# A two-layer hybrid trunk on one core: the first modulation group k tile by k tile, and the next layer's preparation behind the last residual sums

## The chip, the core and the metric

The kernel runs on one core of a Trainium2 chip. The metric is device time in microseconds of one execution; the profile's span, from the first to the last instruction, is a little shorter. The engines are TensorE (PE; its weight loads are listed as PEld), VectorE (DVE), ScalarE (ACT), GpSimd (POOL) and SyncE (SP), which issues nearly all DMAs. Each engine works through its own queue in order; the queues wait for each other by semaphores. VectorE, ScalarE and TensorE work on SBUF and PSUM, GpSimd on SBUF.

## The reference: what is computed

x is 256 tokens by 2048 float32; there are two layers. The core of a layer is:

```python
shift, scale, gate = split(silu(c) @ w_ada[l] + b_ada[l], 3)        # 2048 -> 3 x 2048, for one row c
h = rms_norm(x, norm_w[l]) * (1 + scale) + shift
(gq, gk, gv, glr, gz, dq, dk, dv, da, db, dz, aq, ak, av, az) = split(h @ w_in[l])   # 2048 -> 7704
o_gla  = gated linear attention(gq, gk, gv, glr), normed, times silu(gz)      # 512 wide
o_gdn  = gated delta rule(dq, dk, dv, da, db), normed, times silu(dz)         # 512 wide
o_diff = differential softmax attention(aq, ak, av), normed, times silu(az)   # 1024 wide
x = x + gate * (concat(o_gla, o_gdn, o_diff) @ w_out[l])                      # 2048 -> 2048
```

## The kernel before, in words

x lies transposed: 128 features on the partitions, 16 k tiles of 128 features, 256 tokens along the row. All large weights come from memory once, as tiles of 128x1024 float32 (512 KB), through one pool of six buffers (`wraw`, tag `raw`) that projection weights (`raw`), output weights (`raw`) and modulation weights (`rawa`) share in program order.

Products keep float32 accuracy by splitting both factors: `weights` (L292 to L303) issues the DMA on SP, ScalarE rounds to the fast format (`wh`, L300) and VectorE takes the rest (`wl`, L301), into three buffers each. Each product is then three matmuls: high by high, high by low, low by high. The modulated input is split in the same way into `hh` (ScalarE, L389) and `hl` (VectorE, L390).

The modulation vectors come from `ada_group`: a group is eight VectorE products of a 128x1024 tile with the broadcast `c_row`, each with a running sum (L325), and four small ScalarE finishes (L337). Groups 0 to 7 of a layer give scale and shift of two k tiles each, groups 8 to 11 the gate. Layer 0's first group uses two separate buffers `fr`, the others `raw` buffers. `ada_to(n)` emits products up to mark n (eight per group, 96 per layer); `ADA_BY` and `PACE` say how far the products have to be at the end of each projection step and how they are spread over the 48 columns of the output projection. In a product's place in the program order the scheduler may still move it: `high_priority(offset=AHEAD)` lets it go before other work.

A layer begins with `rstd_rows` (ones-matmuls over the squares, mean, power, two diagonal matrices on ScalarE, a matmul that spreads the row factors over the partitions, a copy to `rb`), then `modulate` for pairs of k tiles (hn, hh, hl: L388 to L390), then `project` for each entry of `STEPS`, a range of output blocks and of k tiles. Layer 0's first step is blocks 18 to 27 (ten of 512 columns) over k tiles 0 and 1: its first chunk of weights holds two blocks for k tile 0, the second the same blocks for k tile 1, the others one block for both. Every chunk is 12 matmuls of 512 columns. In layer 1 the first step spans k tiles 0 to 7, a chunk being one block for two k tiles. `pt` is the PSUM tile of these matmuls.

The heads run as generators between the matmuls. The output projection has three phases (GLA, GDN, differential attention; `py` is its PSUM tile) of 16 columns each; every column ends in a residual sum on VectorE (`xr`, L1183) and, in layer 0, in the last phase, a square on ScalarE (L1191) for the next layer's row statistics. In the last phase of layer 0 each column takes one weight tile and 24 matmuls of 256 columns.

At the start, SP issues the loads in this order: parameters `pt`, c, the identity, x in four quarters, the eight `fr`; ScalarE squares each quarter of x (L1065), GpSimd folds the squares (L1066, L1068), and c is spread to `c_row` by TensorE (`c_ps`) and copied by VectorE and ScalarE in turn.

The order on each engine is made at build time: the program order with priorities, arranged on the framework's own timeline. `in_order()` fixes the order of the instructions inside it on the named engines.

Of the kernel before, what the change touches and what calls it, by code (L numbers as in the profile page):

```python
# [22 lines left out]
L = 2  # L23
# [52 lines left out]
def in_chunks(layer, i):  # L76

    b0, b1, k0, k1 = STEPS[layer][i]
    out = []
    for b in range(b0, b1):  # L80
        for k in range(k0, k1):
            c = out[-1] if out else None
            if c is None or BLOCKS[c[-1][0]][0] != BLOCKS[b][0] or (k == k0 and BLOCKS[b][0] == "T") \
                    or _chunk_elems(c) + _width(b) > RAW:
                out.append([(b, k, k + 1)])
            elif c[-1][0] == b:
                c[-1] = (b, c[-1][1], k + 1)
            else:
                c.append((b, k, k + 1))
# [51 lines left out]
def hybrid_trunk(ctx: ExitStack, tc: tile.TileContext, x, cvec, pos, par, w_ada, w_in, w_out, w_lr, qkn, adt, cst, out):  # L141
# [91 lines left out]
    in_order = lambda: tc.manual_schedule(engines={mybir.EngineType.PE})  # L233
# [3 lines left out]
    SP.dma_start(pt, par)  # L237
# [8 lines left out]
    SP.dma_start(ct[:, 0:128], cst[:, 0:128])  # L246
# [3 lines left out]
    first_raws = []  # L250
    for q in range(2):
        fr = t16("fr", [P, 4, 1024])
        for i in range(4):
            SP.dma_start(fr[:, i, :], w_ada[0, 0, 4 * q + i])
            first_raws.append(fr[:, i, :])
# [14 lines left out]
    nlam = const.tile([P, L], F32, name="nlam")  # L270
    ACT.activation(c16, c16, AF.Silu)
    pr = tiny("lp", 2 * L)
    lam = pcol("lam", 0, 4 * L).rearrange("p (m two) -> p m two", two=2)
    DVE.tensor_tensor(pr.rearrange("p (m o) -> p m o", o=1), lam[:, :, 0:1], lam[:, :, 1:2], ALU.mult)
    pb = bank("lam_ps", "a")
    mm(pb[:, 0:2 * L], ones, pr)
    el = tiny("el", 2 * L)
    ACT.activation(el, pb[:, 0:2 * L], AF.Exp)
    for l in range(L):
        init = 0.8 - 0.6 * math.exp(-0.3 * l)  # L280
        DVE.scalar_tensor_tensor(nlam[:, l:l + 1], el[:, 2 * l + 1:2 * l + 2], -init, el[:, 2 * l:2 * l + 1],
                                 ALU.add, ALU.subtract)
    for i in range(4):
        cb = bank("c_ps", "p")
        for j in range(4):
            mm(cb[:, 128 * j:128 * j + 128], ident[0:KT, 4 * i + j:4 * i + j + 1].broadcast_to([KT, P]), c16)
        (ACT.copy if i % 2 else DVE.tensor_copy)(c_row[:, 512 * i:512 * i + 512], cb)


    state = {"n": 0}  # L290

    def weights(src, n):  # L292

        raw = wraw.tile([P, RAW], F32, name="raw", tag="raw")[:, 0:n]
        wh = wsp.tile([P, RAW], F32R, name="wh", tag="wh")[:, 0:n]
        wl = wsp.tile([P, RAW], F32R, name="wl", tag="wl")[:, 0:n]
        with tc.high_priority(offset=AHEAD if state["n"] else 0):
            SP.dma_start(raw, src)
        with tc.high_priority(offset=AHEAD):
            ACT.copy(wh, raw)  # L300
            DVE.tensor_tensor(wl, raw, wh.bitcast(F32), ALU.subtract)  # L301
        state["n"] += 1
        return wh, wl  # L303

# [3 lines left out]
    DVE.tensor_scalar(pcol("b_ada", 0, 48 * L), pcol("b_ada", 0, 48 * L), 0.5, None, ALU.mult)  # L308
# [4 lines left out]
    def ada_group(l, g, raws=None):  # L313

        sums = tiny("ada_p", 8)
        for i in range(8):
            if raws is None:
                raw = wraw.tile([P, RAW], F32, name="rawa", tag="raw")[:, 0:1024]
                with tc.high_priority(offset=AHEAD):
                    SP.dma_start(raw, w_ada[l, g, i])  # L320
            else:
                raw = raws[i]
            cb = c_row[:, 1024 * (i % 2):1024 * (i % 2) + 1024]
            with tc.high_priority(offset=AHEAD):
                DVE.scalar_tensor_tensor(raw, raw, 1.0, cb, ALU.mult, ALU.mult, accum_out=sums[:, i:i + 1])  # L325
            if i < 7:
                yield
        for f in range(4):
            if g < 8:
                k = 2 * g + f % 2  # L330
                j = 0 if f < 2 else 1
            else:
                k = 4 * (g - 8) + f
                j = 2
            o, scale = ada[l][:, j, k:k + 1], pcol("norm", 16 * l + k) if j == 0 else 1.0
            bias = pcol("b_ada", 48 * l + (16, 0, 32)[j] + k)
            ACT.activation(tiny("ada_j", 2), sums[:, 2 * f:2 * f + 2], AF.Identity, bias=bias, scale=scale, accum_out=o)  # L337
        yield

    def ada_all():  # L340
        for l in range(L):
            for g in range(12):
                yield from ada_group(l, g, first_raws if l == 0 and g == 0 else None)

    ada_it = ada_all()
    ada_n = [0]
# [14 lines left out]
    def rstd_rows(sqs):  # L361
# [21 lines left out]
    def modulate(l, xt, rb, hh, hl, k):  # L383

        for i in range(k, k + 2):
            h = reg(i % 4, "hn")[:, 0:T]
            scale, shift = ada[l][:, 0, i:i + 1], ada[l][:, 1, i:i + 1]
            DVE.scalar_tensor_tensor(h, rb, scale, xt[:, i, :], ALU.mult, ALU.mult)  # L388
            ACT.activation(hh[:, i, :], h, AF.Identity, bias=shift)  # L389
            DVE.scalar_tensor_tensor(hl[:, i, :], h, shift, hh[:, i, :].bitcast(F32), ALU.add, ALU.subtract)  # L390


    in_off = [0]
# [24 lines left out]

    def project(l, group, hh, hl, o, after):
# [18 lines left out]
        for chunk in in_chunks(l, group):  # L438
            n = _chunk_elems(chunk)
            src = w_in[in_off[0]:in_off[0] + P * n].rearrange("(p n) -> p n", p=P)  # L440
            in_off[0] += P * n
# [846 lines left out]
```

## Time and profile before

| | before |
|---|---|
| median of 3 runs | 1101.14 us (1100.52 to 1104.81) |
| the profiled execution | 1103.98 us, span 1102.2 us |
| TensorE busy, share of the span | 1047.0 us, 95% |
| VectorE | 888.6 us, 81% |
| ScalarE | 607.2 us, 55% |
| GpSimd | 219.8 us, 20% |
[...]
| read from memory | 267.76 MB |

Busy time counts the instructions themselves, not register work, semaphores or the issue of DMAs. Matmuls overlap in TensorE's pipeline, so the time between the starts of two is shorter than the time of one.

### The profile page before, as it was taken

The numbers are of one execution on the slowest core, as the hardware profiler recorded it, in microseconds if no ns is written. First come the engines' busy times: TensorE is split into PE (matmuls) and PEld (weight loads), VectorE is DVE, ScalarE is ACT, GpSimd is POOL, SyncE is SP. The second block draws the span as 40 slices with busy tenths as digits, with TensorE's granted clock in tenths as the row PEclk, the third lists the DMA queues.
The fourth block names the chain that finished last, engine by engine and source line by source line (L and its number), as shares of the span: only waits on it lengthen the run. The fifth ranks groups of instructions, "written<-read, shape, count | busy, mean of one in ns | idle before, by whom it ended". The sixth has DMA issues, their size and how long they took to land.

```text
span 1102.2 us, 19699 instructions
## 1 busy us (share of the span) xinstructions
PE 1047.0 (95%) x7398; PEld 918.9 (83%) x7398; DVE 888.6 (81%) x1365; ACT 607.2 (55%) x1251; POOL 219.8 (20%) x284
## 2 busy tenths in 40 slices
PE   4999999999899989999979999999999999999998
PEld 3768888889898777898977877899989877889998
DVE  5899999998999886888687776677756776787874
ACT  4745544447765646466545555468444556557742
POOL 4000000040130841134210000024222144102400
PEclk9999999999999999999998999999999999999999
DMA  9888999999877545755588888796535645777472
GB/s 352 311 299 308 351 336 341 329 296 339 301 270 254 182 145 188 249 162 186 167 318 327 308 315 319 238 306 228 181 116 174 218 164 172 246 244 236 136 216 90
DMA packets 76799, 273.24 MB, mean 248 GB/s; under 512 B 8816, under 2 KB 9888, under 8 KB 76576
## 3 DMA queue, kind: packets, MB, share of 16 engines
q1 hardware_dynamic: 76704, 271.99, 71.7%
q8 instruction: 58, 0.95, 0.3%
q14 instruction: 37, 0.30, 0.1%
HBM read 267.76 MB, written 4.19 MB: 247 GB/s over the span
## 4 chain that ended last, share of the span: by engine, by line
PE 55%; DVE 18%; DMA 11%; issue 9%; ACT 5%; POOL 2%; SPq 0%; DVEq 0%; ACTq 0%; POOLq 0%
PE pt L180 20%; PE py L180 12%; PE pf L180 12%; DMA rawa<-in_w_ada 8%; DVE wl L301 6%; DVE rawa L325 5%; DMA raw<-in_w_in 2%; ACT wh L300 2%; PE Z_ps L180 1%; PE o_gdn L180 1%; DVE fr L325 1%; PE s_ps L180 1%; DVE aqk L436 1%; DVE z L436 1%; PE o_diff L180 1%
## 5 line engine op out<-in xcount | busy, mean ns | idle before, releaser
L300 ACT CAST wh<-raw 128x1024 fp32r<-128x1024 f32 (+1 forms) x312 | 320.0, 1028 | 272.9 <-PE pt L180 119.4
L301 DVE TENSOR_TENSOR wl<-raw,wh 128x1024 fp32r<-128x1024 f32 (+1 forms) x312 | 384.1, 1236 | 72.2 <-ACT wh L300 68.9
L180 PE MATMUL pt<-wl,hh 128*128 128x512 f32 (+1 forms) x768 | 293.5, 383 | 5.4 <-DVE wl L301 5.4
L180 PE MATMUL pt<-wh,hl 128*128 128x512 f32 (+1 forms) x768 | 291.7, 382 | 0.0
L325 DVE SCALAR_TENSOR_TENSOR rawa<-rawa,c_row 128x1024 f32<-128x1024 f32 x184 | 229.1, 1250 | 74.6 <-DMA rawa<-in_w_ada 74.3
L180 PE MATMUL pt<-wh,hh 128*128 128x512 f32 (+1 forms) x768 | 273.1, 383 | 8.5 <-ACT hh L389 4.3
L180 PEld LDWEIGHTS pt<-wh,hh 128*128 128x128 f32 x768 | 145.3, 191 | 40.6 <-ACT hh L389 5.7
L180 PEld LDWEIGHTS pt<-wl,hh 128*128 128x128 f32 x768 | 145.9, 190 | 38.3 <-DVE wl L301 10.4
L180 PEld LDWEIGHTS pt<-wh,hl 128*128 128x128 f32 x768 | 146.0, 190 | 28.7 <-issue 0.2
L180 PE MATMUL pf<-hh,wl 128*128 128x256 f32 x512 | 143.4, 283 | 3.5 <-DVE wl L301 3.5
L180 PE MATMUL pf<-hh,wh 128*128 128x256 f32 x512 | 144.3, 282 | 1.7 <-ACT wh L300 1.6
L180 PE MATMUL pf<-hl,wh 128*128 128x256 f32 x512 | 144.1, 282 | 0.0
L180 PE MATMUL py<-ogg,wh 128*128 128x256 f32 x512 | 101.1, 291 | 1.2 <-DVE xr L1183 0.6
L180 PEld LDWEIGHTS pf<-hh,wl 128*128 128x128 f32 x512 | 95.6, 188 | 6.0 <-DVE wl L301 4.2
L180 PEld LDWEIGHTS pf<-hh,wh 128*128 128x128 f32 x512 | 96.1, 188 | 3.1 <-ACT wh L300 1.8
L180 PEld LDWEIGHTS pf<-hl,wh 128*128 128x128 f32 x512 | 96.0, 188 | 1.5 <-issue 1.0
L180 PE MATMUL py<-odf,wh 128*128 128x256 f32 x512 | 91.4, 282 | 1.4 <-ACT odf L1028 1.0
L180 PEld LDWEIGHTS py<-ogg,wh 128*128 128x128 f32 x512 | 81.4, 190 | 3.2 <-DVE xr L1183 0.8
L180 PEld LDWEIGHTS py<-odf,wh 128*128 128x128 f32 x512 | 79.0, 190 | 2.5 <-ACT odf L1028 1.5
L337 ACT ACTIVATE ada_j<-ada_p,pt 128x2 f32<-128x2 f32 x96 | 31.1, 324 | 80.5 <-DVE rawa L325 72.8
L180 PE MATMUL py<-odf,wl 128*128 128x256 f32 x256 | 71.9, 282 | 1.4 <-DVE wl L301 1.3
L180 PE MATMUL py<-ogg,wl 128*128 128x256 f32 x256 | 72.7, 285 | 0.0
(277 smaller groups left out, 1335.9 us busy)
## 6 DMA issues: line engine op xcount, KB each, us to landing
raw<-in_w_in SPq DMA_DIRECT2D x224, 512.0 KB, 4.8
rawa<-in_w_ada SPq DMA_DIRECT2D x184, 512.0 KB, 4.8
raw<-in_w_out SPq DMA_DIRECT2D x64, 512.0 KB, 4.2
raw<-in_w_in SPq DMA_DIRECT2D x20, 402.0 KB, 4.4
fr<-in_w_ada SPq DMA_DIRECT2D x8, 512.0 KB, 10.6
xt<-in_x SPq DMA_DIRECT2D x4, 512.0 KB, 5.6
xr<-in_x SPq DMA_DIRECT2D x4, 512.0 KB, 8.2
xs<-xr SPq DMA_DIRECT2D x1, 2048.0 KB, 10.2
```

The lines of the kernel that those rows point to most:

```text
L180: return PE.matmul(o, lhsT=lhsT, rhs=rhs, start=start, stop=stop, **kw)
L300: ACT.copy(wh, raw)
L301: DVE.tensor_tensor(wl, raw, wh.bitcast(F32), ALU.subtract)
L325: DVE.scalar_tensor_tensor(raw, raw, 1.0, cb, ALU.mult, ALU.mult, accum_out=sums[:, i:i + 1])
L337: ACT.activation(tiny("ada_j", 2), sums[:, 2 * f:2 * f + 2], AF.Identity, bias=bias, scale=scale, accum_out=o)
L436: DVE.tensor_tensor(d, src, d, ALU.add)
```

## The change: what it does

The parts, with the diff's core behind them:

- Loads at the start: the identity and the parameters are issued on ScalarE's queue, no longer on SP's. SP issues c, x, then four `fr` tiles, a first projection tile, four `fr` tiles, a second projection tile. The `fr` tiles come in the order 0, 1, 4, 5, 2, 3, 6, 7, so that scale and shift of k tile 0 come before those of k tile 1.
- The folds of the squares run on VectorE, with one more fold, so that the row statistics need one matrix instead of two. All four copies to `c_row` run on VectorE. The first halving of `b_ada` and one small product of the lambda part run on GpSimd; the lambda part is queued behind the last fold, the last square and the last spread matmul.
- `rstd_rows`: the two diagonals, their matmul and the copy are replaced by two matmuls with r broadcast as the stationary operand and the identity as the moving one; `rb` stays in PSUM.
- Layer 0's first group is written out by hand in a fixed order for VectorE and ScalarE: products 0, 1, 4, half a cast, product 5, then k tile 0's modulation, with the other casts, product 2 and the first weight split between its hh and its hl; then products 3, 6, 7 and k tile 1's modulation with the second split.
- The large constants load behind the last weight tile of layer 0's first step, no longer in front of its second block.
- Between the layers: `PACE` is 46 instead of 48 and layer 0 goes on to mark (1, 3) instead of (1, 2), eight products more. Products emitted in the last four columns are queued behind that column's residual sum; layer 1's first weight tile is cast behind the last square and split behind the last sum; k tiles 0 and 1 of layer 1 are modulated first, and the products and casts of the first step are queued behind them. `issue_after(i)` adds only an order on i's own engine.

The diff, cut to what the prediction speaks of:

```diff
+    if (layer, i) == (0, 0):
+
+        out = [[(b0, k, k + 1), (b0 + 1, k, k + 1)] for k in range(k0, k1)]
+        b0 += 2
...
+    ACT.dma_start(ct[:, 0:128], cst[:, 0:128])
+    ACT.dma_start(pt, par)
...
+            n = 4 * (i // 2) + 2 * q + i % 2
+            SP.dma_start(fr[:, i, :], w_ada[0, 0, n])
+            first_raws[n] = fr[:, i, :]
+        load_first()
...
+    behind = {}
+
+    def queued(what):
+        return tc.issue_after(behind[what].ins) if what in behind else nullcontext()
...
     def weights(src, n):
 
         raw = wraw.tile([P, RAW], F32, name="raw", tag="raw")[:, 0:n]
+        with tc.high_priority(offset=AHEAD):
+            last_dma[0] = SP.dma_start(raw, src)
         wh = wsp.tile([P, RAW], F32R, name="wh", tag="wh")[:, 0:n]
         wl = wsp.tile([P, RAW], F32R, name="wl", tag="wl")[:, 0:n]
-        with tc.high_priority(offset=AHEAD if state["n"] else 0):
-            SP.dma_start(raw, src)
         with tc.high_priority(offset=AHEAD):
-            ACT.copy(wh, raw)
-            DVE.tensor_tensor(wl, raw, wh.bitcast(F32), ALU.subtract)
-        state["n"] += 1
+            with queued("cast"):
+                ACT.copy(wh, raw)
+            with queued("split"):
+                DVE.tensor_tensor(wl, raw, wh.bitcast(F32), ALU.subtract)
         return wh, wl
...
+    def ada_product(raw, i, sums):
+        cb = c_row[:, 1024 * (i % 2):1024 * (i % 2) + 1024]
+        with tc.high_priority(offset=AHEAD), queued("ada"):
+            DVE.scalar_tensor_tensor(raw, raw, 1.0, cb, ALU.mult, ALU.mult, accum_out=sums[:, i:i + 1])
...
-        dg = reg(8, "dg")[:, 0:T]
-        pb = bank("rstd_ps", "a")
-        rb = small.tile([P, T], F32, name="rb", tag="rb", bufs=1)
+        rb = bank("rstd_ps", "a")[:, 0:T]
         with tc.high_priority(offset=AHEAD):
             ACT.activation(m, ss[:, 0:2], AF.Identity, bias=eps, scale=1.0 / D)
             row_power(r, m, 2)
             for t in range(2):
-                ACT.activation(dg[:, 128 * t:128 * t + 128], ident, AF.Copy, scale=r[:, t:t + 1])
-            mm(pb[:, 0:T], ones, dg)
-            ACT.copy(rb, pb[:, 0:T])
+                mm(rb[:, 128 * t:128 * t + 128], r[:, t:t + 1].broadcast_to([P, P]), ident)
         return rb
...
+    def modulate(l, xt, rb, hh, hl, k, between=lambda: None):
+
+        h = reg(k % 4, "hn")[:, 0:T]
+        scale, shift = ada[l][:, 0, k:k + 1], ada[l][:, 1, k:k + 1]
+        DVE.scalar_tensor_tensor(h, rb, scale, xt[:, k, :], ALU.mult, ALU.mult)
+        modulated = ACT.activation(hh[:, k, :], h, AF.Identity, bias=shift)
+        between()
+        split = DVE.scalar_tensor_tensor(hl[:, k, :], h, shift, hh[:, k, :].bitcast(F32), ALU.add, ALU.subtract)
+        return split, modulated
...
+            wh, wl = done_first.pop(0) if done_first else chunk_weights(n)
...
     sqx = t16("sqx", [P, KT, T])
-    for q in range(4):
-        p = sqx[:, 4 * q:4 * q + 4, :]
-        ACT.activation(p, xt0[:, 4 * q:4 * q + 4, :], AF.Square)
-        POOL.tensor_tensor(p[:, 0:2, :], p[:, 0:2, :], p[:, 2:4, :], ALU.add)
-        if q > 0:
-            POOL.tensor_tensor(sqx[:, 0:2, :], sqx[:, 0:2, :], p[:, 0:2, :], ALU.add)
-    sq = [sqx[:, 0, :], sqx[:, 1, :]]
+    with tc.high_priority(offset=2 * AHEAD):
+        for q in range(4):
+            p = sqx[:, 4 * q:4 * q + 4, :]
+            squared = ACT.activation(p, xt0[:, 4 * q:4 * q + 4, :], AF.Square)
+            DVE.tensor_tensor(p[:, 0:2, :], p[:, 0:2, :], p[:, 2:4, :], ALU.add)
+            if q > 0:
+                DVE.tensor_tensor(sqx[:, 0:2, :], sqx[:, 0:2, :], p[:, 0:2, :], ALU.add)
+        last_fold = DVE.tensor_tensor(sqx[:, 0, :], sqx[:, 0, :], sqx[:, 1, :], ALU.add)
...
+        if l > 0:
+            done_first.append(chunk_weights(_chunk_elems(in_chunks(l, 0)[0])))
...
+            sums = tiny("ada_p", 8)
+
+            def product(n):
+                ada_product(first_raws[n], n, sums)
+                if n % 2 == 1:
+                    ada_finish(0, 0, sums, n // 2)
+
+            first = [[wsp.tile([P, RAW], F32R, name=n, tag=n) for n in ("wh", "wl")] for _ in range(2)]
+
+            def cast(i, a, z):
+                ACT.copy(first[i][0][:, a:z], loaded[i][:, a:z])
+
+            def split(i):
+                DVE.tensor_tensor(first[i][1], loaded[i], first[i][0].bitcast(F32), ALU.subtract)
+                done_first.append(first[i])
+
+            def meanwhile(i):
+                if i == 0:
+                    cast(0, 512, RAW)
+                    cast(1, 0, RAW)
+                    product(2)
+                split(i)
+
+            with tc.high_priority(offset=AHEAD), in_order(mybir.EngineType.DVE, mybir.EngineType.Activation):
+                with tc.issue_after(last_fold.ins):
+                    product(0)
+                product(1)
+                product(4)
+                cast(0, 0, 512)
+                product(5)
+                modulate(0, xt, rb, hh, hl, 0, lambda: meanwhile(0))
+                for n in (3, 6, 7):
+                    product(n)
+                modulate(0, xt, rb, hh, hl, 1, lambda: meanwhile(1))
+            mod[0] = 2
+
+        else:
+            with tc.high_priority(offset=AHEAD):
+                for k in range(2):
+                    behind["ada"], behind["cast"] = modulate(l, xt, rb, hh, hl, k)
+            mod[0] = 2
+
         for i, (b0, b1, k0, k1) in enumerate(STEPS[l]):
+            if l == 0 and i == 1:
+                with tc.issue_after(last_dma[0].ins):
+                    load_constants()
...
+            behind.clear()
...
+            squared = ACT.activation(s, xr[:, c, :], AF.Square)
+            if c >= 12:
+                behind["ada"] = summed
+            if c == KT - 1:
+                behind["split"], behind["cast"] = summed, squared
...
-PACE = 48
+PACE = 46
 
 QKL = 3
 
-ADA_BY = {0: ((0, 1), (0, 2), (0, 3), (0, 5), (0, 7), (0, 11), (1, 0), (1, 2)), 1: ((1, 7), (1, 9), (1, 11))}
+ADA_BY = {0: ((0, 1), (0, 2), (0, 3), (0, 5), (0, 7), (0, 11), (1, 0), (1, 3)), 1: ((1, 7), (1, 9), (1, 11))}
```

## Rows read from the trace of the kernel before

**Rows 1.** The page: busy us, share of the span and instructions of each engine.

```profile
PE 1047.0 (95%) x7398; PEld 918.9 (83%) x7398; DVE 888.6 (81%) x1365; ACT 607.2 (55%) x1251; POOL 219.8 (20%) x284
```

**Rows 2.** Busy us by stage: PE, PEld, DVE, ACT, POOL; clock, DMA share, GB/s.

```profile
0.00:20.00 20.00, 9.30 (x42) 8.95 (x42) 9.38 (x18) 8.60 (x12) 10.92 (x13) 1.00 0.88 330
20.00:40.00 20.00, 14.44 (x52) 10.90 (x53) 16.47 (x28) 12.11 (x27) 0.97 (x1) 1.00 0.93 346
...
560.00:580.00 20.00, 12.97 (x92) 11.86 (x91) 19.70 (x29) 8.93 (x23) 2.08 (x3) 0.84 0.98 364
```

**Rows 3.** Timeline of the start: start us, us, engine, line, out<-in [idle before].

```profile
0.72 1.28 ACT L271 ACT_TABLE_LOAD   x1 [0.72 <-PEq L1276]
...
11.60 1.06 ACT L1065 ACTIVATE sqx<-xt 128x1024 f32<-128x1024 f32 x1 [1.42 <-DMA xt<-in_x]
...
12.88 1.61 SPq L298 DMA_DIRECT2D raw<-in_w_in  x2
12.99 2.08 DVE L325 SCALAR_TENSOR_TENSOR fr<-fr,c_row 128x1024 f32<-128x1024 f32 x1 [3.18 <-DMA fr<-in_w_ada]
13.96 4.45 POOL L1068 TENSOR_TENSOR sqx<-sqx 128x512 f32<-128x512 f32 x2
...
15.45 0.33 SPq L320 DMA_DIRECT2D rawa<-in_w_ada  x1
...
19.42 1.22 DVE L325 SCALAR_TENSOR_TENSOR fr<-fr,c_row 128x1024 f32<-128x1024 f32 x1
...
27.11 1.22 PE L180 MATMUL pt<-wh,hh 128*128 128x512 f32 x2 [2.75 <-ACT hh L389]
```

**Rows 4.** Timeline of the change of layer, by engine.

```profile
572.57 2.34 DVE L301 TENSOR_TENSOR wl<-raw,wh 128x1024 fp32r<-128x1024 f32 x2
574.84 0.47 DVE L1183 SCALAR_TENSOR_TENSOR xr<-py,ada,xr 128x256 f32<-128x256 f32 x1
...
578.48 0.69 ACT L378 ACTIVATE dg<-ct,rs 128x128 f32<-128x128 f32 x2 [0.82 <-POOL rs L359]
...
580.48 0.37 ACT L380 COPY rb<-rstd_ps 128x256 f32<-128x256 f32 x1 [0.75 <-PE rstd_ps L180]
...
570.96 0.28 PE L180 MATMUL py<-odf,wl 128*128 128x256 f32 x1
...
575.49 1.86 PE L180 MATMUL ss<-ones,sq 128*128 128x1 f32 x8 [2.76 <-ACT sq L1191]
579.22 1.22 PE L180 MATMUL rstd_ps<-dg,ones 128*128 128x256 f32 x2 [1.87 <-ACT dg L378]
581.97 0.79 PE L180 MATMUL pt<-wh,hh 128*128 128x512 f32 x1 [1.52 <-ACT hh L389]
```

**Rows 5.** Groups of VectorE's instructions, 553 to 581 us: busy us, mean ns.

```profile
L325 DVE SCALAR_TENSOR_TENSOR rawa<-rawa,c_row 128x1024 f32<-128x1024 f32 x12 | 16.1, 1352 | 2.9 <-DMA rawa<-in_w_ada 2.8
```

**Rows 6.** Busy time by stage, in four other stretches, columns as in rows 2.

```profile
30.00:57.50 27.50, 27.50 (x118) 22.09 (x117) 21.64 (x30) 20.71 (x39) 0.00 (x0) 1.00 0.85 314
57.50:100.00 42.50, 38.64 (x194) 30.59 (x193) 41.67 (x62) 19.25 (x35) 0.00 (x0) 1.00 0.83 281
...
440.00:553.00 113.00, 109.02 (x843) 102.64 (x842) 89.97 (x171) 63.46 (x149) 33.95 (x62) 0.97 0.59 196
...
562.00:571.00 9.00, 7.49 (x62) 7.02 (x60) 9.00 (x14) 2.75 (x8) 1.07 (x1) 1.00 0.93 342
```

**Rows 7.** Groups of VectorE's instructions, 440 to 572 us.

```profile
L325 DVE SCALAR_TENSOR_TENSOR rawa<-rawa,c_row 128x1024 f32<-128x1024 f32 x21 | 27.7, 1327 | 8.0 <-DMA rawa<-in_w_ada 8.0
L1183 DVE SCALAR_TENSOR_TENSOR xr<-py,ada,xr 128x256 f32<-128x256 f32 x46 | 21.8, 475 | 8.2 <-PE py L180 8.1
...
L925 DVE TENSOR_TENSOR scr<-scr 128x512 f32<-128x512 f32 x1 | 0.7, 693 | 0.1
```

**Rows 8.** Busy time behind the restart, columns as in rows 2.

```profile
582.00:587.00 5.00, 5.00 (x12) 3.93 (x13) 5.00 (x14) 2.98 (x7) 0.00 (x0) 0.50 0.96 398
```

**Rows 9.** The chain of work that ended last: start us, us, what.

```profile
27.11 27.13 PE pt L180 x108
```

More of the change, by code (lines that the diff above doesn't have):

```diff
@@ L1 @@
 import math
-from contextlib import ExitStack
+from contextlib import ExitStack, nullcontext
 import numpy as np
@@ L249, in hybrid_trunk, with load_first @@
         SP.dma_start(xt0[:, 4 * q:4 * q + 4, :], x[:, 4 * q:4 * q + 4, :])
-    first_raws = []
+    first_raws, loaded, in_off = {}, [], [0]
+    def load_first():
+        raw = wraw.tile([P, RAW], F32, name="raw", tag="raw")
+        SP.dma_start(raw, w_in[in_off[0]:in_off[0] + P * RAW].rearrange("(p n) -> p n", p=P))
+        in_off[0] += P * RAW
+        loaded.append(raw)
     for q in range(2):
@@ L269, in hybrid_trunk @@
     junk_n = [0]
-    nlam = const.tile([P, L], F32, name="nlam")
     ACT.activation(c16, c16, AF.Silu)
[L272 to L282, printed above, removed]
     for i in range(4):
@@ L311, in hybrid_trunk, with ada_finish, ada_group @@
                                  ALU.add, ALU.mult)
-    def ada_group(l, g, raws=None):
+    def ada_product(raw, i, sums):
+        cb = c_row[:, 1024 * (i % 2):1024 * (i % 2) + 1024]
+        with tc.high_priority(offset=AHEAD), queued("ada"):
+            DVE.scalar_tensor_tensor(raw, raw, 1.0, cb, ALU.mult, ALU.mult, accum_out=sums[:, i:i + 1])
+    def ada_finish(l, g, sums, f):
+        if g < 8:
+            k = 2 * g + f % 2
+            j = 0 if f < 2 else 1
+        else:
+            k = 4 * (g - 8) + f
+            j = 2
+        o, scale = ada[l][:, j, k:k + 1], pcol("norm", 16 * l + k) if j == 0 else 1.0
+        bias = pcol("b_ada", 48 * l + (16, 0, 32)[j] + k)
+        with queued("cast"):
+            ACT.activation(tiny("ada_j", 2), sums[:, 2 * f:2 * f + 2], AF.Identity, bias=bias, scale=scale, accum_out=o)
+    def ada_group(l, g):
         sums = tiny("ada_p", 8)
         for i in range(8):
[L317 to L323, printed above, removed]
+            raw = wraw.tile([P, RAW], F32, name="rawa", tag="raw")[:, 0:1024]
             with tc.high_priority(offset=AHEAD):
-                DVE.scalar_tensor_tensor(raw, raw, 1.0, cb, ALU.mult, ALU.mult, accum_out=sums[:, i:i + 1])
+                SP.dma_start(raw, w_ada[l, g, i])
+            ada_product(raw, i, sums)
             if i < 7:
@@ L328, in ada_group @@
         for f in range(4):
[L329 to L337, printed above, removed]
+            ada_finish(l, g, sums, f)
         yield
@@ L342, in ada_all @@
             for g in range(12):
-                yield from ada_group(l, g, first_raws if l == 0 and g == 0 else None)
+                if (l, g) != (0, 0):
+                    yield from ada_group(l, g)
     ada_it = ada_all()
-    ada_n = [0]
+    ada_n = [8]
     def ada_to(n):
@@ L1100, in block_done @@
             lo, hi = span
-            if l == 0 and b == STEPS[0][0][0] and len(seen) == 0:
-                seen.add("constants")
-                load_constants()
             advance(lo + int((hi - lo) * done))
```

55 lines of the change are left out of this document (30 added, 25 removed).

## The prediction, on record before the changed kernel's time was known

> **What bounds the kernel now.** I read the page first: TensorE is busy 95% of the span and VectorE 81% [rows 1], so a change that leaves the matmuls as they are can win only TensorE's idle time, 1102.2 - 1047.0 = 55.2 us, and its time at half clock. Then the busy time by stage [rows 2], to see where those 55 us lie. Two places stand out. In the first 20 us TensorE has 9.30 us of work, and that is preparation; in the next 20 it idles 5.6. At the change of layer it idles 7.0 us between 560 and 580, at a mean granted clock of 0.84. The diff edits both places.
>
> The order of time at the start comes next [rows 3]. The reader is to see a line of waits: the last quarter of x is squared from 11.60 to 12.66 us, GpSimd folds the squares until 18.41, VectorE multiplies eight tiles of the first modulation group, and only after the eighth come the first two hn, so the first projection matmul starts at 27.11. VectorE's first product takes 2.08 us while GpSimd folds, and one after the folds 1.22.
>
> At the change of layer [rows 4] the last output-projection matmul ends at 571.24 (570.96 + 0.28), but the last residual sum, which it feeds, starts at 574.84: two weight splits stand ahead of it on VectorE. Then come square, ones-matmuls, mean, power, two diagonals, a matmul, a copy, hn and hh, and TensorE restarts at 581.97, 10.7 us after it ran dry. Twelve adaLN products run on VectorE from 553 to 581 [rows 5]. It is the full engine there: from 562 to 571 it is busy 9.00 us of 9 and TensorE 7.49 [rows 6], so TensorE loses 1.5 us before it runs dry.
>
> **The change, part by part: the start.** The squares' folds go from GpSimd to VectorE, where a 128x512 sum costs 0.69 us [rows 7]. Only what follows the last square counts: two such sums and a 256-wide one (0.48, as a residual sum [rows 7]), with overlap some 1.8 us. The five earlier folds, and the two c_row copies that leave ScalarE, lie where VectorE waits for data; were they not hidden, they would cost seven times 0.69, 4.8 us. Two small loads leave SP's queue, so x is issued sooner by two issues, 0.7 us by the 0.33 of the issues shown [rows 3]. Bounds: nothing to 0.7. I take 0.4, since the transfers too fill the time until 11.60. The last square then ends at 12.3 and the folds at 14.1.
>
> Products 0, 1, 4, 5 follow at 1.15 us from start to start (1.22 less the overlap; two splits of that size take 2.34 [rows 4]): 18.7. They give scale and shift of k tile 0. hn and hh, half a us each, bring TensorE's start to about 19.6 instead of 27.11. The row statistics run meanwhile: two ones-matmul pairs, mean, power and broadcast take less than 3.5 us after the folds, so rb is there at 17.5, a good us before hn asks. In that slack the lambda work hides too, which moves behind the last square with its activation-table load; if the slack were gone, it would cost that load, 1.28 us [rows 3].
>
> The first chunk has 12 matmuls, at half clock 0.42 us each (12 in 5.00 [rows 8]). Four start at once; the low part waits for product 2 and the split (21.4), so the chunk ends at 24.8. The second chunk needs four more products and the second weight tile. SP's issues at 12.88 and, third, 15.45 each wait for a landing [rows 3]: a 512 KB tile every 1.28 us, the first at 12.9. In the new order the second raw tile is the tenth, 12.9 - 0.4 + 9 x 1.28 = 24.0. Its cast, about 1.1 us with the hop, which stands ahead of the second hh on ScalarE, ends at 25.1; two small finishes, hn and hh bring the second start to 26.2. At full clock a matmul takes 27.5 / 118 = 0.233 us [rows 6], twelve end at 29.0. In before, the chain's first stretch of 108 matmuls ends at 27.11 + 27.13 = 54.24 [rows 9], so its 24th was done 84 x 0.233 earlier, at 34.7. The gain at that point is 5.7 us, or 3.5 if the second chunk runs at half clock (31.2).
>
> Will it be kept? From 30 to 57.5 TensorE is full and VectorE idles 27.5 - 21.64 = 5.9; the DMA engines are 0.85 busy, which leaves 4.1 us [rows 6]. The constants' 512 KB move out of this stretch, one interval of 1.28 more. From 57.5 to 100 VectorE is the bound (41.67 of 42.5), so the lead lives on only if VectorE has it too, and it has the 5.9. I take 4.5 us, with 3.5 and 5.7 as ends, and nothing if VectorE or the transfers give no room (a rival below).
>
> Cost at nothing: b_ada's halving on GpSimd (under 1.3 us, a fold's time, and wanted only by the first finish near 16 us), the later constants (wanted by the head groups, long after 100 us), and rb read from PSUM (the residual sum reads PSUM and takes 0.475 [rows 7]).
>
> **The change of layer.** Eight adaLN products more are spread over the output projection (from mark 104 to 128 in 46 steps, before to 120 in 48), and those of its last four columns stand behind the residual sums. The eight were the ones issued ahead of layer 1's modulation, so of the twelve late products about four remain. VectorE's load per column of the last phase is then a split 1.15, a sum 0.40 and half a product 0.6, together 2.15 us, against TensorE's 24 matmuls at 0.117, 2.8 (half the columns of the 0.233 ones). TensorE bounds, and its 1.5 idle us go: it runs dry at 569.7. The eight cost 9.2 us of VectorE between 440 and 553, where it idles 113 - 89.97 = 23.0 [rows 6].
>
> From there the chain is that of before, 574.84 to 581.97, 7.13 us, less the two diagonals (0.69), the copy (0.37), their two hops (0.1) and half of eight ones-matmuls (0.93, or 0.6 if they overlapped the square): 5.0 to 5.4. The broadcast matmuls take at most the old pair's 1.22 and, at half its columns, at least 0.6. I take 5.4 in all. Against 10.7 that is 5.3; with the 1.5 it is 6.8 us.
>
> What is late next: in before, three weight tiles were split ahead of the restart; now only the first is, and the others stand behind the second hh. If VectorE does eight hn and eight hl (16 x 0.40 = 6.4 us from 574.1) before the second split (1.15), the second chunk's low part waits until 581.7. TensorE has 20 matmuls until then, the first chunk and the high parts of the second: from 575.1 to 583.5 at half clock, to 579.8 at full. So 0 to 1.9 us is given back; I take 1.3. Gain 5.5, ends 4.9 and 6.8.
>
> **Sum.** 4.5 + 5.5 = 10.0 us of the profiled execution's 1103.98 (its span is 1102.2): 1094.0. The median of the runs, 1101.14, lies 0.26% below that execution; in the same proportion I forecast 1091.2.
>
> [...] The change starts TensorE early and then lets it pause, 1.4 us between the first chunk and the second. [...]
>
> **The rivals.**
> [...]
> Start absorbed: VectorE's full stretch from 57.5 to 100, or the transfers, give no room and the 4.5 us vanish: 1095.7. For it 41.67 of 42.5, against it the 5.9 us just before.
> Change of layer absorbed: late splits starve TensorE in the first chunks of layer 1 and give the 5.5 back: 1096.7. Against it, the 20 matmuls of cover.
> No effect: the engines' other orders cancel both gains: 1101.
> Slower: the eight added products hold up VectorE's queue in the output projection. It is in order, so a product that waits for its tile holds the sums and splits behind it. In before 21 products wait 8.0 us there [rows 7], 0.4 each, hidden by three split buffers. To end 0.5% above before, 10.0 + 5.5 us must reach TensorE, 1.9 for each of the eight, five times that: 1107 or more.
> [...]
>
> **How the numbers follow.** Forecast 0.50, clock 0.12, start absorbed 0.12, change of layer absorbed 0.09, no effect 0.05, slower 0.07, more 0.05. A measurement of this kernel tells about 0.5%, 5.5 us, from no change, so below 1095.6 is faster. Forecast, clock and more lie below it and start absorbed on the line, split in half: faster 0.73. Same: 0.06 + 0.09 + 0.05 = 0.20. Slower 0.07. The range 1086 to 1098 leaves out no effect and slower (0.12) and some tails of the others.
>
> **What would show it.** First projection matmul at 19 to 21 us and a pause of 1 to 2 us near 25; products of 1.2 us from the first, and no fold on GpSimd; about four products in VectorE's last 25 us before the restart; the restart 5 to 6 us behind the last output matmul. Wrong: the 24th projection matmul after 32 us; TensorE idle 2 us or more in the 20 us behind the restart; its idle time from 440 to 553, now 113 - 109.02 = 4.0, longer by several us.

## The result, and the profile after

The changed kernel takes 1113.57 us (median of 6 runs, 1112.07 to 1114.44); the kernel before took 1105.96 on the same chip (1100.52 to 1108.79). The ratio is 1.0077 [1.0048, 1.0106]: slower, where 1091.2 us and a ratio of 0.991 were forecast. The profiled execution spans 1111.7 us, 9.5 more than before's.

The page first, busy us and share of the span by engine, against [rows 1]: TensorE has 7.2 us more busy time for the same 7398 matmuls. Its mean granted clock is 0.982, where before had 0.988.

```profile
PE 1054.2 (95%) x7398; PEld 921.3 (83%) x7398; DVE 891.8 (80%) x1373; ACT 604.8 (54%) x1244; POOL 218.5 (20%) x279
```

Busy time by stage, columns as in [rows 2] and [rows 6], with 313 to 440 us added (layer 0's heads):

```profile
20.00:40.00 20.00, 18.55 (x68) 13.59 (x68) 19.20 (x30) 13.84 (x27) 0.00 (x0) 1.00 0.98 358
313.00:440.00 127.00, 119.56 (x1079) 98.92 (x1079) 112.24 (x167) 68.58 (x183) 48.28 (x41) 0.96 0.64 209
440.00:553.00 113.00, 98.85 (x724) 90.75 (x723) 82.20 (x162) 55.71 (x140) 29.11 (x56) 0.91 0.52 169
553.00:585.00 32.00, 32.00 (x274) 32.00 (x273) 21.54 (x30) 14.46 (x25) 11.75 (x9) 1.00 0.77 254
592.00:597.00 5.00, 5.00 (x13) 3.93 (x12) 5.00 (x10) 3.38 (x8) 0.00 (x0) 0.50 0.62 222
```

The two edited places do what was forecast. TensorE has 18.55 us of work in the second 20 us, where it had 14.44 [rows 2], and from 553 to 585 it never idles. The loss is elsewhere. From 440 to 553, where TensorE idled 4.0 us [rows 6], it idles 113 - 98.85 = 14.15, and the granted clock is 0.91 for 0.97.

The start, timeline of VectorE and TensorE, against [rows 3], and the chain, against [rows 9]:

```profile
13.49 0.42 DVE L1086 TENSOR_TENSOR sqx<-sqx 128x256 f32<-128x256 f32 x1
13.83 1.22 DVE L327 SCALAR_TENSOR_TENSOR fr<-fr,c_row 128x1024 f32<-128x1024 f32 x1
...
19.68 2.07 PE L184 MATMUL pt<-wh,hh 128*128 128x512 f32 x4 [1.63 <-ACT hh L401]
...
26.27 1.20 PE L184 MATMUL pt<-wh,hh 128*128 128x512 f32 x4 [1.45 <-ACT hh L401]
...
29.52 0.50 PE L184 MATMUL pt<-wh,hh 128*128 128x512 f32 x1
```

```profile
26.27 23.25 PE pt L184 x96
```

The folds end on VectorE at 13.91 and the next product takes 1.22 us. The first projection matmul starts at 19.68 (27.11 before), the second chunk at 26.27, the third at 29.52. The chain's first long stretch ends at 26.27 + 23.25 = 49.52, 4.7 us sooner than 54.24 [rows 9].

The change of layer, timeline, against [rows 4], and VectorE's products from 553 to 592, against [rows 5]:

```profile
584.95 0.28 PE L184 MATMUL py<-odf,wl 128*128 128x256 f32 x1
...
585.27 0.48 DVE L1260 SCALAR_TENSOR_TENSOR xr<-py,ada,xr 128x256 f32<-128x256 f32 x1 [2.34 <-PE py L184]
...
587.73 1.29 POOL L376 TENSOR_TENSOR rs<-ms,mhalf 128x2 f32<-128x2 f32 x1 [10.94 <-ACT ms L390]
...
589.08 1.22 PE L184 MATMUL rstd_ps<-ct,rs 128*128 128x128 f32 x4 [1.72 <-POOL rs L376]
...
591.41 0.80 PE L184 MATMUL pt<-wh,hh 128*128 128x512 f32 x1 [1.12 <-ACT hh L401]
```

```profile
L327 DVE SCALAR_TENSOR_TENSOR rawa<-rawa,c_row 128x1024 f32<-128x1024 f32 x4 | 4.9, 1221 | 2.1 <-DMA rawa<-in_w_ada 2.1
```

Between the end of the last output matmul (585.23) and the restart lie 6.2 us, where there were 10.7; the residual sum starts as its matmul ends, with no split ahead of it, and four products are left of twelve. But all of this comes 14 us later than before: 584.95 for 570.96 [rows 4]. Behind the restart TensorE has a granted clock of 0.50 and 13 matmuls in 5.00 us (592 to 597 us), as in [rows 8].

So a lead of 4 to 5 us turned into a lag of 14 between 315 and 585 us, in layer 0's heads and output projection. TensorE's matmuls by tile show where (duration in ns, first and last start):

```profile
L184 PE MATMUL G_ps<-fm x32: 222/222/270, 311.7 to 315.5; 128*64 128x64 f32 x32
L184 PE MATMUL Y_ps<-Um,C x160: 218/218/366, 348.2 to 416.6; 64*64 64x64 f32 x160
L184 PE MATMUL u_ps<-vb,fm x16: 270/275/348, 431.5 to 442.5; 128*128 128x128 f32 x16
L184 PE MATMUL s_ps<-aqk x48: 270/275/417, 481.0 to 507.1; 128*128 128x128 f32 x48
```

G_ps opens the delta rule's inverse, Y_ps is in its five levels, u_ps is the first use of it, s_ps the first tile of the softmax heads. In before these tiles started at 315.6, 346.0 (last 403.1), 421.4 and 467.7. The inverse's last Y_ps comes 13.5 us late although G_ps comes 3.9 early. The order of the projection matmuls `pt` in TensorE's queue is another. Rows of `pt` alone, from the first G_ps to the first Y_ps and from the first u_ps on, before and then after:

```profile
315.50:345.90 30.40, 0.89 (x2) 1.00 0.77 260
421.40:440.00 18.60, 10.80 (x42) 1.00 0.56 185
```

```profile
311.70:348.10 36.40, 6.36 (x25) 1.00 0.79 260
431.40:450.00 18.60, 0.00 (x0) 0.91 0.77 288
```

Of the 240 `pt` matmuls of this stage 25 now run ahead of the first Y_ps, where 2 did, and none is left behind u_ps, where 42 were. The first Y_ps comes 36.5 us behind the first G_ps instead of 30.4, and TensorE is busy for 36.0 us of it: the lead goes without idle time. What follows u_ps then has no projection matmuls beside it, and there, from 440 to 553, the 14.15 us of idle time lie.

The other engines' orders differ too. What TensorE waited for from 313 to 553 (total, times, longest), and its timeline in the middle of the inverse:

```profile
PE oT_ps L188 <- DVE z L1034: 3.8, 2, 2.2
PE Y_ps L184 <- DVE Um L809: 3.7, 1, 3.7
PE aT_ps L188 <- DVE scr L981: 3.1, 2, 2.9
```

```profile
384.83 1.10 PE L184 MATMUL Z_ps<-Tm,Y 64*64 64x64 f32 x32
...
390.87 0.40 PE L184 MATMUL pt<-wh,hh 128*128 128x512 f32 x1
394.92 0.33 PE L184 MATMUL Y_ps<-Um,C 64*64 64x64 f32 x4 [3.66 <-DVE Um L809]
395.44 0.66 PE L188 MATMUL ropeT_ps<-ct,scr 128*128 128x128 f32 x4 [0.18 <-DVE scr L941]
396.02 0.54 PE L184 MATMUL Y_ps<-Um,C 64*64 64x64 f32 x8
```

After Z_ps of the third level TensorE has 22 projection matmuls `pt` (12 in before); then it stands 3.66 us for Um, and the next level's Y_ps alternate with rope transposes that stand between them in its queue. Um is late on VectorE, where it stands behind a rope step that waits for GpSimd's `mix`; in before Um, at 383.65, goes ahead of that step (392.98):

```profile
392.54 0.76 DVE L939 TENSOR_TENSOR scr<-aqk,rtab 128x256 f32<-128x256 f32 x2 [5.60 <-POOL mix L660]
...
394.36 0.41 DVE L809 TENSOR_TENSOR Um<-Um,Z_ps 128x256 f32<-128x256 f32 x1
```

One pause of this size is not the difference, though: before has one too, in the fourth level, for a rope transpose.

```profile
PE ropeT_ps L184 <- DVE scr L925: 3.4, 1, 3.4
```

GpSimd's queue is reordered as well: the third of its level masks C (L799) stands behind the norms of q and k (`r_d`, L376), where in before it goes, at 380.28, ahead of the last two of them.

```profile
379.62 2.54 POOL L376 TENSOR_TENSOR r_d<-r_d,mhalf 128x8 f32<-128x8 f32 x1
...
390.22 1.29 POOL L799 TENSOR_TENSOR C<-Lm,ct 128x512 f32<-128x512 f32 x1
```

No line of the heads is in the diff, which touches of this stage only the weight loads and the added products; run 9 has neither of these edits. The instructions are else those of before; their order in the queues is another.

### The profile page after: what moved, and what is told of

It reads as the page before. It is cut to its first block, busy times and chain, and to the rows that moved or that the text cites. A ratio compares the mean times of both kernels' runs of the same rounds, so it can differ in the third digit from the quotient of the medians.

```text
span 1111.7 us, 19676 instructions
## 1 busy us (share of the span) xinstructions
PE 1054.2 (95%) x7398; PEld 921.3 (83%) x7398; DVE 891.8 (80%) x1373; ACT 604.8 (54%) x1244; POOL 218.5 (20%) x279
## 4 chain that ended last, share of the span: by engine, by line
PE 49%; DVE 22%; DMA 11%; issue 10%; POOL 4%; ACT 4%; DVEq 0%; ACTq 0%; POOLq 0%; SPq 0%
PE pt L184 18%; PE py L184 15%; DMA rawa<-in_w_ada 8%; PE pf L184 7%; DVE wl L311 7%; DVE rawa L327 7%; DMA raw<-in_w_in 2%; ACT wh L309 1%; DVE on_gdn L673 1%; DVE z L454 1%; DVE aqk L454 1%; PE o_diff L184 1%; PE o_gdn L184 1%; PE Z_ps L184 1%; PE s_ps L184 1%
## 5 line engine op out<-in xcount | busy, mean ns | idle before, releaser
L309 ACT CAST wh<-raw 128x1024 fp32r<-128x1024 f32 (+2 forms) x310 | 317.9, 1028 | 285.3 <-PE pt L184 123.2
L311 DVE TENSOR_TENSOR wl<-raw,wh 128x1024 fp32r<-128x1024 f32 (+2 forms) x310 | 382.0, 1238 | 62.1 <-ACT wh L309 61.5
```

## The experiments

Every ratio is against the kernel before, run on the same chip between the others, with its 95% interval.

**1 to 3: one part alone.** First the change of layer alone:

```diff
-PACE = 48
+PACE = 46
...
-ADA_BY = {0: ((0, 1), (0, 2), (0, 3), (0, 5), (0, 7), (0, 11), (1, 0), (1, 2)), 1: ((1, 7), (1, 9), (1, 11))}
+ADA_BY = {0: ((0, 1), (0, 2), (0, 3), (0, 5), (0, 7), (0, 11), (1, 0), (1, 3)), 1: ((1, 7), (1, 9), (1, 11))}
...
+            if c >= 12:
+                behind["ada"] = summed
+            if c == KT - 1:
+                behind["split"], behind["cast"] = summed, squared
...
+            done_first.append(chunk_weights(_chunk_elems(in_chunks(l, 0)[0])))
```

> The kernel before with only the change-of-layer part (eight products more ahead of it, the queueing behind the last residual sums, layer 1's first tile and modulation first); the start and the row statistics are those of before. Theory (GpSimd's order in layer 0's heads, set by the start part, costs the time): 4 to 6 us faster than before, ratio 0.994 to 0.997, because GpSimd's queue keeps the order of before. Rival A (the eight products hold VectorE up in the output projection): about 10 us slower, ratio 1.005 or more. Rival B (VectorE's or DMA order, not GpSimd's): as the theory.

Measured: 1.008 [1.0051, 1.0109]; the theory, GpSimd's order set by the start part, missed. The last output matmul starts at 580.4, 9.4 us late, the lag growing from 433 us on. That has the sign and the place of the recorded rival; whether its mechanism too is the question of runs 10 and 11. Then the changed kernel with these lines taken back, so the start alone:

> The changed kernel with the change-of-layer part taken out (120 marks in 48 steps, no queueing behind sums, no first tile or modulation ahead); the row statistics stay in their new form. Theory: the lead of 5 us at the start is lost and 13 us more with it by 540 us, ratio 1.010 to 1.014, since GpSimd's queue has the order of the changed kernel. Rival A: 4 to 5 us faster, 0.995 to 0.997. Rival B: slower as the theory.

Measured: 1.0135 [1.0104, 1.0166]. The first s_ps starts at 480.2. Then the changed kernel without the eight products (`PACE` 48, mark (1, 2)):

> The changed kernel with marks and steps of before (120 in 48), so without the eight products more in the output projection; all else stays. Theory: slower than before as the changed kernel is, 1.005 to 1.012, with the eight back on the path at the change of layer adding up to 5 us. Rival A: the output projection recovers, ratio 0.995 or less.

Measured: 1.0083 [1.0052, 1.0114]. The restart comes 6.1 us sooner than in the changed kernel (585.3 for 591.4), but layer 1 takes 6.1 longer to its last `pt` (421.9 for 415.8), all of it by the first `pf` tile (150.0 us behind the restart for 143.7): the eight come back in its first step. Taking them away wins nothing.

**4: GpSimd's queue set by hand.** In the changed kernel the norms of k and the scaling of q stand behind the masks:

```diff
+        late = l == 0 and a == 1
+        if late:
+            yield lambda: g.levels == 5
...
+            with tc.issue_after(g.level.ins) if late else nullcontext():
+                POOL.tensor_scalar(r, r, 1.0 / 128.0, EPS, ALU.mult, ALU.add)
+                row_power(r, r, 8)
```

> The changed kernel with GpSimd's queue in layer 0's heads held: the norms of ak and the scaling of q come behind the fifth level mask of the inverse. Theory: the third mask on GpSimd no longer waits behind them, its start comes 10 us earlier, and the gains at the two edited places show: 5 to 10 us faster than before, ratio 0.991 to 0.996. Rival A and rival B: no better than the changed kernel by more than 3 us, 1.004 or more.

Measured: 1.0038 [1.0018, 1.0058]. The theory missed. The last Y_ps moved only from 416.6 to 413.8 and s_ps was later still (484.6). GpSimd's place is part of it at most: with its queue free, the third mask came 2.9 us sooner, not 10, and the last two masks waited for TensorE's Y_ps. TensorE's order had stayed: 25 `pt` matmuls ahead of the first Y_ps, 2 behind u_ps.

**5 to 7: the order held.** These take the built order of one kernel and hold another's instructions in it, on TensorE, VectorE, ScalarE and GpSimd, from layer 0's first head to the end of the second output phase. `HELD` lists positions; the edges order issue on an engine and add no wait for data.

```diff
+HELD = {
...
+def hold(nc, tc):
...
+        for p, q in zip(order, order[1:]):
+            tc.add_manual_dep(mine[q], mine[p].name,
+                              mybir.DependencyInfo(mybir.DependencyClass.NoSync, mybir.DependencyReason.DATA), reason="hold")
...
         hybrid_trunk(tc, *args)
+        hold(nc, tc)
```

The start alone, in before's order:

> The start part alone (change of layer as before), with the instructions of TensorE, VectorE, ScalarE and GpSimd that belong to layer 0's heads and to the first two phases of its output projection held in the order in which the kernel before has them; that is an order only, no instruction and no wait for data is added. Theory (the loss is the order that the build gave this unedited stage): the lead of 4 to 5 us at the first G_ps lives on, the first s_ps starts near 463 where the start part alone had 480 and before 467.7, and the whole is 3 to 5 us below before, ratio 0.995 to 0.998. Rival (the earlier start itself makes the stage longer, by transfers or VectorE's load, whatever the order): s_ps stays near 478 to 480 and the ratio at 1.010 or more. Between 466 and 476: both have a share.

Measured: 0.9949 [0.9925, 0.9973], where the same instructions in their own order gave 1.0135. G_ps starts at 311.2 and s_ps at 466.7, 1.0 ahead of before and not 5. By the marks set for this run (466 to 476) the rival has a share at this point: the lead is still 3.8 us at u_ps and shrinks behind it. By the restart it is 3.1 (578.9 for 582.0). The kernel before, unchanged, in the start part's order:

> The kernel before, unchanged but for the order: the same instructions (heads of layer 0, first two phases of its output projection) are held in the order in which the start part alone has them. Theory (order): with nothing edited, the stage from the first G_ps to the first s_ps takes 165 to 171 us instead of 152, and the whole is 10 to 17 us above before, ratio 1.009 to 1.016. Rival (the earlier start itself): the stage stays within 3 us of before's 152 and the ratio within 1.003.

Measured: 1.0154 [1.0129, 1.018]. With nothing edited but the order, the inverse is as late as in the changed kernel, and two of its long waits come back (316 to 553 us):

```profile
L180 PE MATMUL Y_ps<-Um,C x160: 218/218/366, 352.0 to 418.4; 64*64 64x64 f32 x160
L180 PE MATMUL u_ps<-vb,fm x16: 272/275/275, 435.2 to 436.9; 128*128 128x128 f32 x16
```

```profile
PE Y_ps L180 <- DVE Um L793: 3.9, 1, 3.9
PE aT_ps L184 <- DVE scr L965: 3.5, 1, 3.5
```

From G_ps to s_ps it takes 167.9 us, where before takes 152.1 and the changed kernel 169.3. Last the whole change in before's order:

> The whole change, with the same instructions held in the order of the kernel before; the eight products added to the output projection are placed by the build where they fall. Theory (order for the heads, and the eight products for the output projection): the lead is there at the first u_ps (416 to 418, in after 431.5), the products then cost up to 9 us until the first rstd_ps, and the change of layer gives 4 back: 0 to 5 us below before, ratio 0.995 to 1.000. If the eight cost only through the order that they bring, held away here: both gains are seen whole, 8 to 10 us below before, ratio 0.991 to 0.993. If order is not the cause: 1.006 or more.

Measured: 0.9935 [0.9915, 0.9955], 1096.33 us beside 1102.63: the same edits, faster than both kernels. Tiles, stages and GpSimd's third mask:

```profile
L184 PE MATMUL Y_ps<-Um,C x160: 218/218/267, 343.9 to 401.7; 64*64 64x64 f32 x160
L184 PE MATMUL u_ps<-vb,fm x16: 274/275/275, 420.0 to 421.6; 128*128 128x128 f32 x16
```

```profile
313.00:440.00 127.00, 123.01 (x1149) 102.88 (x1149) 109.52 (x164) 70.97 (x184) 46.23 (x41) 0.97 0.65 203
440.00:553.00 113.00, 104.84 (x807) 97.60 (x806) 95.23 (x181) 62.11 (x155) 37.60 (x62) 0.98 0.69 215
581.40:586.40 5.00, 3.59 (x15) 2.59 (x15) 5.00 (x9) 1.75 (x3) 0.00 (x0) 1.00 0.85 292
```

```profile
377.91 2.28 POOL L799 TENSOR_TENSOR C<-Lm,ct 128x512 f32<-128x512 f32 x1
```

The third mask starts at 377.91 instead of 390.22, and u_ps 14.9 us before the last `pt` matmul (434.9), which covers the recurrence behind it. In the changed kernel u_ps starts 1.0 us after the last `pt` (430.5): the cover was spent ahead of it. TensorE's idle time from 313 to 553 is 7.4 + 14.15 = 21.6 us there, 4.0 + 8.2 = 12.2 here and 8.9 in before.

The two counts of `pt` sort all runs. With the start's edits or run 9's, and in run 6, 25 run ahead of the first Y_ps and at most 2 behind u_ps; in before, in the held runs 5, 7, 11 and 12, and with the change of layer alone (1, 8, 10), it is 2 and 42 or 43. The change of layer alone therefore loses its time another way, behind u_ps.

**8: the change of layer without the eight products**, on the kernel before.

> The change of layer alone on the kernel before, without the eight products: the start is before's, the products go to the old mark at the old pace, and only the queueing behind the last sums, the first tile and the two k tiles modulated ahead are changed. Theory (the eight products make the loss of the change of layer alone, 9.5 us up to the last output matmul): the last py start is within 2 us of before's 570.8, the restart comes 3 to 5 us sooner than 582.0, and layer 1 takes 4 to 7 us more for the eight products that come back in its first step: ratio 0.999 to 1.003. Rival (the queueing costs in the output projection, not the products): last py near 578 to 580 and a ratio of 1.006 or more.

Measured: 1.0082 [1.0057, 1.0106]. Half of the theory held: the last output matmul is at 568.7 and the restart at 575.9, 6.1 us sooner. Layer 1 then takes 15.0 us more, not 4 to 7. Busy time 5 to 15 us behind the restart:

```profile
580.90:590.90 10.00, 1.54 (x5) 0.55 (x3) 10.00 (x21) 6.37 (x15) 0.00 (x0) 0.66 0.93 326
```

VectorE is full with products and modulations, its next weight split comes only at 589.57, and TensorE has 1.54 us of work in 10. That is 9.2 of the 15 by the first `pf` tile (153.6 us behind the restart, 144.4 before); the rest is lost in layer 1's heads and was not traced further. Without the eight ahead of it, the queueing pays for them behind the restart.

**9: two issues moved**, on the kernel before:

```diff
-    SP.dma_start(pt, par)
...
-    SP.dma_start(ct[:, 0:128], cst[:, 0:128])
+    ACT.dma_start(ct[:, 0:128], cst[:, 0:128])
+    ACT.dma_start(pt, par)
```

> The kernel before with one edit of the first microsecond and nothing else: the parameters and the identity are issued on ScalarE's queue instead of SP's, as in the change. By the trace that saves two issues, under 0.7 us at the start; but the build then orders layer 0's heads much as it does for the start part alone. Theory (order): the start is within 1 us of before's, the stage from the first G_ps to the first s_ps takes 162 to 171 us instead of 152, and the ratio is 1.008 to 1.016. Rival (the loss needs the change's own work, its products, folds or queueing): the ratio is 0.998 to 1.002.

Measured: 1.0211 [1.0187, 1.0236], more than the theory's 1.016.

The first G_ps starts at 320.6 and the first s_ps at 489.4: the stage takes 168.8 us, as forecast, in the order that the start part has (25 and 2 `pt` matmuls, as counted above). The start, forecast level, is 3.0 us late as well; the last section has its cause.

**10 and 11: the eight products in before's order.** The change of layer alone again, and held as in runs 5 to 7:

> The change of layer alone on the kernel before, once more as in the first group, as the partner of the next run on the same chip. Both theories expect what it gave there: ratio 1.005 to 1.011, the first s_ps near 472.7 and the last output matmul near 580.

> The change of layer alone on the kernel before, with the eight products, and the instructions of layer 0's heads and of the first two output phases held in the order of the kernel before. Theory (the eight products cost nothing themselves; what the change of layer alone lost in the output projection was the order that they brought): the first s_ps is within 1.5 us of before's 467.7, the last output matmul starts by 572, and the whole is 2 to 5 us below before, ratio 0.995 to 0.998. Rival, the one of the prediction (the eight products hold up VectorE's queue in the output projection): s_ps near 472, the last output matmul near 580, ratio 1.005 or more.

Measured: 1.0096 [1.0072, 1.012] as built, 0.9994 [0.9979, 1.001] held. Held, s_ps starts at 468.9 and the last output matmul at 572.2 (584.6 as built), with the eight in place: 19 products lie between 440 and 553 us, where before has 12. They do not hold up VectorE's queue by themselves; what the order they brought cost, the old order gives back. The gain missed: the restart comes 2.2 us sooner than in before and layer 1 takes 3.5 more, which was not traced.

**12: TensorE's queue alone held**, in the start part:

> The start part alone, with TensorE's queue alone held in the order of the kernel before over layer 0's heads and the first two output phases; VectorE, ScalarE and GpSimd are left to the build, which then follows nearly. If TensorE's order decides: as with all four held, the first s_ps near 466 and a ratio of 0.994 to 0.998. If another queue decides (GpSimd's, as the run with its norms queued behind the masks supposed): s_ps at 472 or later and a ratio of 1.003 or more.

Measured: 0.9987 [0.9968, 1.0007]; s_ps at 470.3. Between the two: of the way from 1.0135 to 0.9949, TensorE's order alone brings 0.0148 of 0.0186, 80%. The other engines' orders were free to follow it, so the 80% are not TensorE's queue by itself.

First start of three tiles, last start of py and first matmul of layer 1 by run (us, views by tile); lag is that of the last output matmul behind before's. Each row is one execution, and a difference of 1 or 2 us between two rows shows nothing: at G_ps, ahead of which their edits are alike, the kernels with the start's edits lie between 310.9 and 313.5, those with before's start between 315.6 and 317.6 (run 9 apart).

| kernel | G_ps | u_ps | s_ps | last py | restart | lag | ratio |
|---|---|---|---|---|---|---|---|
| before | 315.6 | 421.4 | 467.7 | 571.0 | 582.0 | | |
| changed | 311.7 | 431.5 | 481.0 | 585.0 | 591.4 | 14.0 | 1.0077 |
| start alone | 310.9 | 431.8 | 480.2 | 583.4 | 593.9 | 12.4 | 1.0135 |
| start, before's order | 311.2 | 417.6 | 466.7 | 568.5 | 578.9 | -2.5 | 0.9949 |
| before, start's order | 316.1 | 435.2 | 484.0 | 585.7 | 596.3 | 14.7 | 1.0154 |
| changed, before's order | 313.5 | 420.0 | 465.4 | 570.0 | 576.5 | -1.0 | 0.9935 |
| two issues moved | 320.6 | 441.5 | 489.4 | 592.2 | 603.1 | 21.2 | 1.0211 |

## Why the prediction was wrong

**The step that failed** is that of "Will it be kept?", where the lead "lives on" if VectorE and the transfers have room. Room was not the condition. The step took the unedited stages as they stand in the trace of before, in its order. The order is made at build time on a planner's timeline of the whole program, and the edit of the first 30 us gave the heads at 316 us another one: 25 `pt` matmuls ahead of the first Y_ps instead of 2, none behind u_ps instead of 42, and a lead of 3.9 us at G_ps became a lag of 13.3 at s_ps. Runs 5 and 6 show it from both sides: before's order gives the start its gain, the start's order costs the kernel before 1.5%. Run 9 shows that little is needed. Why the planner chose this order was not tried.

**The start** was right in mechanism and size: 19.68 (19.6 forecast), second chunk 26.27 (26.2), 24th matmul done as the third chunk starts, 29.5 (29.0); the chain's first stretch ends 4.7 us sooner (4.5). Held in before's order it is worth 0.0051 x 1102.63 = 5.6 us, 3.0 to 8.3.

**The change of layer** was half right. The gap behind the last output matmul is 6.2 us (5.4 forecast; the power, taken as in before, where it was 0.71 us beside products, took 1.29 beside the weight split, and the broadcast matmuls the upper bound, 1.22). "It runs dry at 569.7", 1.5 sooner, is not seen: with the order held the last py starts at 570.0, and without the change of layer (run 5) at 568.5. But run 7 is 2.3 us behind run 5 already at G_ps, 1.2 of it from the second chunk (below); counted from G_ps the last py is 0.8 sooner. The give-back came as forecast: TensorE has 3.59 of 5 us from 581.4 to 586.4 in run 7, 1.4 idle (1.3 taken). Net, run 7's restart is 2.4 us ahead of run 5's and layer 1's last projection matmul (990.9 for 994.2) 3.3, for 5.5 forecast; counted from G_ps it is 4.7 and 5.6. By the ratios, 0.9935 and 0.9949, the two runs are not told apart, so the size of this gain stays open. Held, the sum of 10.0 measures 7.2 us, 5.0 to 9.4.

**The rivals.** "Slower" gave the right sign by luck, with a wrong mechanism. Its mark, longer idle time from 440 to 553, came; but runs 10 and 11 refute the held-up queue, and in run 7 twenty products wait 4.4 us for their tiles, where 21 waited 8.0 [rows 7] (440 to 570 and to 572 us):

```profile
L327 DVE SCALAR_TENSOR_TENSOR rawa<-rawa,c_row 128x1024 f32<-128x1024 f32 x20 | 24.9, 1249 | 4.4 <-DMA rawa<-in_w_ada 4.3
```

"No effect: the engines' other orders" named the right mechanism, with a chance of 0.05, and priced it as if an order could only cancel a gain. An order has a price of its own, up to 17 us here.

**The clock** went both ways. The chances named "clock" and "more" count 2.3 us, twelve matmuls at 0.42 us [rows 8] instead of 0.233 [rows 6], lost in the second chunk or saved behind the restart. This is the author's estimate, and no run shows it: run 7 loses 1.2 us in the second chunk, the other executions with this start nothing, and behind the restart the granted clock is 0.50 in the changed kernel and 0.66 in run 7 (576.4 to 581.4 us). In the changed kernel the twelve matmuls behind the pause of 1.45 us start within 3.25 us (26.27 to 29.52), 0.27 apart, and the row from 25 to 30 us has a granted clock of 1.00. In five of the six other executions with this start the pause is 1.05 to 1.67 us and the outcome the same. In run 7 the pause is 1.78, and the second chunk takes 4.43 us (26.16 to 30.59), with a granted clock of 0.68 in the row from 25 to 30 us:

```profile
26.16 1.55 PE L184 MATMUL pt<-wh,hh 128*128 128x512 f32 x4 [1.78 <-ACT hh L401]
```

```profile
25.00:30.00 5.00, 3.84 (x10) 3.08 (x11) 5.00 (x9) 1.96 (x5) 0.00 (x0) 0.68 0.98 325
```

So a loss behind such a pause does occur, at 1.2 us instead of 2.3 (the third chunk starts at 30.59, in run 5 at 29.43), and in six executions of seven it does not, as idle pieces of 1.5 us in all from 562 to 571 left before's clock at 1.00 [rows 6]. What sets run 7 apart was not shown.

## What to carry to other kernels

Where a scheduler orders the queues, an edit's price includes the new order of every later stage, and that can outweigh the edit: look at an unedited stage first, tile by tile, and ask whether its order is still the old one. Hold the old order in the new kernel, and the new order in the old kernel, before judging the edit: here the same edits were 0.8% slower as built and 0.65% faster held. And find out which chain needs cover: filler matmuls that run ahead of a chain cannot hide it later.

## What the runs showed of the hardware

In run 9, products on VectorE and folds on GpSimd take longer beside each other. On GpSimd and then on VectorE:

```profile
11.99 1.27 POOL L1066 TENSOR_TENSOR sqx<-sqx 128x512 f32<-128x512 f32 x1 [1.64 <-ACT sqx L1065]
13.22 2.24 POOL L1068 TENSOR_TENSOR sqx<-sqx 128x512 f32<-128x512 f32 x1
```

```profile
16.48 2.27 DVE L325 SCALAR_TENSOR_TENSOR fr<-fr,c_row 128x1024 f32<-128x1024 f32 x1
...
23.09 1.21 DVE L325 SCALAR_TENSOR_TENSOR fr<-fr,c_row 128x1024 f32<-128x1024 f32 x1
```

A fold takes 1.27 us while the first product has only begun and 2.24 beside products; a product takes 2.27 beside folds and 1.21 after them. In run 9 the products start while four folds are still to do, so the folds end at 22.07 (18.41 before), and the start is 3.0 us late, not 0.7 early. The changed kernel folds on VectorE, and there the first product already takes 1.22 us (13.83).

The first chunk of the changed kernel took as long as twelve matmuls at a granted clock of 0.50, and its row gives the clock as 1.00 (third number from the end):

```profile
19.60:25.00 5.40, 5.14 (x12) 3.51 (x12) 5.40 (x9) 1.97 (x5) 0.00 (x0) 1.00 1.03 410
```

Twelve matmuls take 5.14 us, as the twelve at 0.50 did [rows 8], and the next twelve 3.25. In before, too, the first nine projection matmuls start within 3.57 us (27.11 to 30.68), 0.45 apart, and the row from 27 to 31 us says 1.00. In these first stretches the matmuls are spaced as at 0.50 (0.42 [rows 8]), and the row gives 1.00; which of the two tells the clock there was not shown.
